# Differential attention: a score map in two PSUM tiles of two and three banks, a constant shift, casts on ACT, less filler per map

## The chip, the cores and the metric

One core of one Trainium2 chip runs the whole program. The metric is the device time of one execution in microseconds. Three executions of the kernel before took 4203.43 (median), 4199.43 and 4225.66 us.

## What is computed

Two layers of a block over 2048 latent and 256 context tokens of width 1024. In each layer one projection feeds four mixers side by side (differential attention, HGRN2, windowed attention with sinks, mLSTM) and a gate; their outputs, times the gate, go through an output projection and are added to the stream. The change lies in the differential attention. Cut to what matters:

```python
def attend(qs, ks, vs):                       # two maps m per head, 4 heads
    s = jnp.einsum('mbhqd,mbhkd->mbhqk', qs, ks).astype(F32) * scale
    p = jax.nn.softmax(s, axis=-1)
    w = (p[0] - lam * p[1]).astype(vs.dtype)
    return jnp.einsum('bhqk,bhkv->bhqv', w, vs)
...
o = lax.map(lambda qq: attend(qq, keys, vals), qb)   # blocks of 128 queries
y = from_heads(rmsnorm(o, g) * (1.0 - lam_init))
```

In the first layer the context tokens attend too (to themselves, 256 keys); in the last layer only the latent ones do, to all 2304 keys.

## The kernel before

Each layer runs in four stretches. First the tokens are normed, transposed and projected for the differential attention alone (`first_blocks`). Then comes the attention, with all other projections as filler for TensorE. Then what is left of the filler runs together with the first tiles of windowed attention and mLSTM (`rest_stream`, `swa_stream`, `mlstm_stream`). Last, HGRN's outputs and the output projection join them.

**A unit.** The attention goes through units: one head and one block of 128 queries. A full unit has 2304 keys, a context unit (two per head, first layer only) 256. Layer 0 has 64 full and 8 context units, layer 1 has 64 full ones. A unit does its two maps one after the other, map 1 first. For each map `diff_scores` writes 128 x 512 scores into one PSUM bank at a time (tile `scr`, a ring of five banks; five matmuls, the last with 256 columns), and VectorE takes each bank's maximum as soon as it is there (line 1048). A last small reduction makes the map's maximum, negated (line 1051). `diff_exp` then runs one exponential per bank on ACT, with the negated maximum as bias and the row sum as an accumulated output, into the SBUF tiles `p` (1024 and 1280 columns). A bank can take scores of the next map when its exponential has read it. For map 0 the bias also holds a term of map 1's row sum, through a reciprocal and a logarithm (lines 1040 to 1043 and 1053).

**Mixing.** `diff_mix` joins the maps a unit later: `p1 * factor + p0` on VectorE (line 1078), the float16 value of it on POOL (line 1080), the rest of it in float16 on POOL (line 1081), and a DMA that transposes both into `wt` (line 1083). It does one half (1024 or 1280 keys) per map. Its VectorE work is put right behind the operation that makes the bias (`issue_after(u["nm"].ins)`). `diff_out` multiplies `wt` by the values into tile `pv`, `diff_norm` scales and norms; they run one unit later again, on `u2` and `u3`.

**Filler.** `pump(ns)` runs steps of the other projections on TensorE until they are worth so many ns by the program's own count of columns. In `diff_scores` it is called after each bank but the last, with FSTEP; behind a map's scores and `diff_out`, with FGAP. Both stand at the end of a row of `ORDER_X`, one row a layer. TensorE's order in the attention is fixed by this code; the other engines' order is set by the scheduler. The filler (`other_blocks`) takes two queues side by side. The heavy one has mLSTM values, windowed keys and queries, mLSTM keys, and last the two gates of HGRN (`hgrn_gates`: twelve or more VectorE, ACT and POOL operations for each 24 pfm matmuls, and state matmuls `ktp` and `dS` behind them). The light one has plain projections and last the gate (`gate_silu`). A token-major projection writes `ptm` (256 columns a matmul), a feature-major one `pfm` (512).

**Behind the attention.** The streams are woven by a table of positions (`ORDER_Y`). While filler is left, windowed attention and mLSTM may only begin two tiles (`room`), since the other tiles' memory is still the projections'.

Of the kernel before, what the change touches and what calls it, by code (L numbers as in the profile page):

```python
# [22 lines left out]
    [33073.0, 2368.0, 1500.0, 1.0, 5637.0, 3547.0, 2, 9000.0, 2653.0, 15000.0, 1.15, 32192.0, 620.0, 2500.0],  # L23
    [29667.0, 2000.0, 2212.0, 1.0, 11215.0, 4000.0, 2, 9000.0, 4000.0, 22918.0, 1.15, 22000.0, 540.0, 2360.0],
# [9 lines left out]
P = 128  # L34
# [20 lines left out]
NEG = -1.0e30  # L55
ZLOW = -80.0
# [11 lines left out]
def kernel(  # L68
# [29 lines left out]
    def act(o, i, f, **kw):  # L98
        A.activation(out=o, in_=i, func=f, **kw)  # L99
# [152 lines left out]
    for l in range(n_layers):  # L252
# [63 lines left out]
        QSC = 32.0 ** -0.5  # L316
# [7 lines left out]
        alam = lp.tile([P, 1], F32, tag="alam", name=f"alam{l}")  # L324
# [11 lines left out]
        with tc.tile_pool(name=f"pa{l}", bufs=2, reuse_waits="tile", side="right" if l else "left") as pa, tc.tile_pool(name=f"pap{l}", bufs=4, space=PSUM, reuse_waits="tile") as pap:  # L336
# [9 lines left out]
            def layer_params():  # L346
# [28 lines left out]
                act(alam, lam, AF.Abs)  # L375
# [643 lines left out]
        with ExitStack() as st2:  # L1019
            da = st2.enter_context(tc.tile_pool(name=f"da{l}", bufs=2, reuse_waits="tile", side="right"))  # L1020
            sps = st2.enter_context(tc.tile_pool(name=f"sps{l}", bufs=1, reuse_waits="tile", space=PSUM, side="right"))
            KCH = [(0, 512), (512, 512), (1024, 512), (1536, 512), (2048, 256)]
            HALF = [(0, 1024), (1024, 1280)]

            def chunks_of(u):
                return [(2048, 256)] if u["ctx"] else KCH

# [3 lines left out]
            def diff_scores(u, m):  # L1031


                ch = chunks_of(u)
                sm = u["sm"]
                mx = sm[:, m * 5:m * 5 + len(ch)]
                pss = u["s", m] = []
                for j, (k0, n) in enumerate(ch):
                    if m == 0 and j == len(ch) - 1:
                        V.tensor_reduce(sm[:, 22:23], sm[:, 15:15 + len(ch)], AX.X, ALU.add)  # L1040
                        V.reciprocal(sm[:, 23:24], sm[:, 22:23])

                        act(sm[:, 24:25], sm[:, 23:24], AF.Ln, scale=alam, bias=one_t)
                    ps = sps.tile([P, 512], F32, tag="sc", name="scr", bufs=5)
                    mm(ps[:, :n], u["Qs"][:, m, u["qo"]:u["qo"] + P], u["Ks"][m][:, k0:k0 + n], True, True)
                    if j < len(ch) - 1:
                        pump(FSTEP * u["work"])
                    V.tensor_reduce(mx[:, j:j + 1], ps[:, :n], AX.X, ALU.max)  # L1048
                    pss.append(ps)
                nm = sm[:, 20 + m:21 + m]  # L1050
                u["nm"] = V.tensor_reduce(nm, mx, AX.X, ALU.max, negate=True)
                if m == 0:
                    u["nm"] = tt(V, nm, nm, sm[:, 24:25], ALU.subtract)

            def diff_exp(u, m):

                sm = u["sm"]
                pt = u[m] = [da.tile([P, 1280], F32, tag=f"p{m}", name=f"p{m}", bufs=4) for _ in halves_of(u)]
                for j, (k0, n) in enumerate(chunks_of(u)):
                    hf = 0 if u["ctx"] or k0 < 1024 else 1  # L1060
                    o = 0 if u["ctx"] else k0 - HALF[hf][0]
                    act(pt[hf][:, o:o + n], u["s", m][j][:, :n], AF.Exp, bias=sm[:, 20 + m:21 + m],
                        accum_out=sm[:, 10 + m * 5 + j:11 + m * 5 + j])

            def diff_mix(u, j):

                sm = u["sm"]
                if j == 0:
                    V.tensor_reduce(sm[:, 25:26], sm[:, 10:10 + len(chunks_of(u))], AX.X, ALU.add)
                    V.tensor_scalar(sm[:, 26:27], sm[:, 25:26], sm[:, 23:24], nlam, ALU.mult, ALU.mult)  # L1070
                    V.reciprocal(sm[:, 27:28], sm[:, 25:26])
                    u["w"] = []
# [5 lines left out]
                stt(p[:, :n], p[:, :n], sm[:, 26:27], u[0][j][:, :n], ALU.mult, ALU.add)  # L1078
                wl = u[0][j].bitcast(F16)
                G.tensor_scalar(wl[:, :n], p[:, :n], one_t, zero_t, ALU.mult, ALU.add)  # L1080
# [640 lines left out]
```

## Time and profile before

| what | us |
|---|---|
| median of 3 executions | 4203.43 |
| profiled execution, its own time | 4224.02 |
| its span, first to last instruction | 4222.2 |
| attention of layer 0 (first to last score matmul) | 238.3 to 1393 |
| attention of layer 1 | 2385 to 3432 |
| TensorE, VectorE, ACT, POOL busy | 3603.4, 3162.2, 2271.5, 2610.5 |

PE is TensorE's matmuls, PEld its weight loads, DVE is VectorE, ACT ScalarE, POOL GpSimd, SP the engine that issues most DMAs. Matmuls are pipelined, so the duration of one is longer than the distance to the next. A line such as L88 or L99 is a helper's; which part of the program it is is seen by the tile names. The granted clock is a share of full speed (2.4 GHz); at its lower level it is 1.2 GHz.

### The profile page before, as it was taken

The page shows a single profiled execution, that of the slowest core. Times are in us where ns is not written, and L with a number is a line of the kernel's source. Part 1 is how long each engine was busy: PE and PEld are TensorE (multiplying, and loading weights), DVE is VectorE, ACT ScalarE, POOL GpSimd, SP SyncE. Part 2 cuts the span into 40 slices and gives each one's busy share as a digit, 9 for nine tenths or more (in the row PEclk, how much of TensorE's full clock was granted, in tenths as well). Part 3 has the DMA queues.
Part 4 walks back from the last instruction along what each step waited for, and adds up shares of the span by engine and source line. Part 5 has one row for each costly group of instructions (what it writes and reads, how often), then busy time and mean ns, then how long its engine had stood idle before and what let it go on. Part 6 is the DMA issues. An engine that isn't in the chain of part 4 may idle for free. (4 is left out here: it accounts for less than half of the span.)

```text
span 4222.2 us, 82225 instructions
## 1 busy us (share of the span) xinstructions
PE 3603.4 (85%) x30342; PEld 2418.7 (57%) x30342; DVE 3162.2 (75%) x6137; ACT 2271.5 (54%) x6105; POOL 2610.5 (62%) x2037
## 2 busy tenths in 40 slices
PE   6999888887778878989998997899877678689998
PEld 3667564555555655655656585545555446556665
DVE  5167777789989776686743498888898986778774
ACT  5244555556666554565633355566666655545553
POOL 4455666555666676686647557775556766556663
PEclk9999899999999958898889999999989889588988
DMA  5357775765665675676644466668765656756662
GB/s 204 101 143 163 161 162 128 168 145 130 153 145 118 169 180 137 161 180 165 170 128 142 122 139 129 145 144 172 153 140 117 132 119 164 184 137 154 166 159 70
DMA packets 1256988, 622.42 MB, mean 147 GB/s; under 512 B 913476, under 2 KB 1203848, under 8 KB 1256584
## 3 DMA queue, kind: packets, MB, share of 16 engines
q1 hardware_dynamic: 1154216, 490.64, 51.8%
q10 hardware_dynamic: 102368, 126.52, 8.9%
q8 instruction: 239, 3.92, 0.4%
q14 instruction: 165, 1.35, 0.1%
HBM read 291.76 MB, written 131.23 MB: 100 GB/s over the span
## 5 line engine op out<-in xcount | busy, mean ns | idle before, releaser
L99 ACT ACTIVATE p<-scr,sm 128x512 f32<-128x512 f32 (+1 forms) x1296 | 814.5, 643 | 335.9 <-DVE sm L102 159.7
L1048 DVE TENSOR_REDUCE sm<-scr 128x1 f32<-128x512 f32 (+1 forms) x1296 | 785.1, 627 | 184.2 <-PE scr L88 175.0
L88 PE MATMUL pfm<-hh,wb 128*128 128x512 f16 (+1 forms) x2592 | 851.6, 376 | 49.6 <-ACT fm L99 12.9
L88 PE MATMUL ptm<-wb,hh 128*128 128x256 f16 (+2 forms) x5024 | 868.3, 276 | 25.5 <-DVE gz L105 7.9
L1080 POOL TENSOR_SCALAR p<-p,one_t,zero_t 128x1024 f16<-128x1024 f32 (+2 forms) x264 | 365.8, 1386 | 574.4 <-ACT p L99 296.4
L88 PE MATMUL ptm<-wb,hl 128*128 128x256 f16 (+2 forms) x2512 | 679.1, 275 | 2.5 <-POOL hl L102 2.4
L88 PEld LDWEIGHTS <-wb 128*128 128x128 f16 x3888 | 383.5, 102 | 519.2 <-issue 167.3
L88 PE MATMUL scr<-Ks,Qs 128*128 128x512 f16 (+1 forms) x1296 | 481.9, 379 | 194.2 <-ACT p L99 193.1
L88 PEld LDWEIGHTS <-hh 128*128 128x128 f16 x5024 | 486.5, 101 | 275.2 <-issue 154.7
L102 POOL TENSOR_TENSOR p<-p,p 128x1024 f16<-128x1024 f32 (+2 forms) x264 | 625.6, 2370 | 16.9
L88 PE MATMUL pfm<-hl,wb 128*128 128x512 f16 (+1 forms) x1296 | 488.2, 377 | 0.0
L105 DVE SCALAR_TENSOR_TENSOR p<-p,sm,p 128x1024 f32<-128x1024 f32 (+2 forms) x264 | 417.6, 1582 | 1.1
L88 PE MATMUL fx<-wo,mh 128*128 128x512 f16 x1088 | 375.5, 430 | 9.4 <-DVE xt L105 4.5
L88 PEld LDWEIGHTS <-hl 128*128 128x128 f16 x2512 | 253.5, 101 | 39.2 <-POOL hl L102 4.5
L88 PE MATMUL pv<-Vs,wt 128*128 128x128 f16 (+1 forms) x4640 | 244.1, 208 | 34.5 <-DMA wt<-p 25.5
L99 ACT ACTIVATION_READ_ACCUMULATOR p<-scr,sm 128x1 f32 x1296 | 267.4, 206 | 0.0
L102 POOL TENSOR_TENSOR ph<-swp,ph 128x640 f16<-128x640 f32 (+2 forms) x136 | 192.7, 1418 | 120.4 <-ACT ph L1322 100.5
L88 PEld LDWEIGHTS <-wt 128*128 128x128 f16 x4640 | 228.5, 99 | 60.3 <-DMA wt<-p 34.1
L88 PE MATMUL fx<-wo,mlo 128*128 128x512 f16 x544 | 233.3, 429 | 20.8 <-DVE mlo L102 20.6
L99 ACT ACTIVATE swp<-ss,ssm 128x640 f32<-128x640 f32 (+2 forms) x136 | 102.9, 756 | 176.5 <-DVE ssm L1318 164.7
L88 PEld LDWEIGHTS <-Qs 128*128 128x128 f16 x1296 | 131.2, 102 | 96.3 <-issue 24.2
L99 ACT ACTIVATE E<-E 128x1024 f32<-128x1024 f32 x119 | 124.8, 1052 | 88.0 <-POOL E L102 41.5
(304 smaller groups left out, 7331.9 us busy)
## 6 DMA issues: line engine op xcount, KB each, us to landing
wraw<-in_w_in_dram SPq DMA_DIRECT2D x60, 512.0 KB
dgt<-ga ACTq DMA_DIRECT2D x68, 256.0 KB
r1b<-dr SPq DMA_DIRECT2D x68, 256.0 KB
gtt<-dgt SPq DMA_DIRECT2D x34, 512.0 KB
mraw<-in_w_mod_dram SPq DMA_DIRECT2D x64, 256.0 KB
vi<-dhi SPq DMA_DIRECT2D x49, 256.0 KB
KSb<-dsk SPq DMA_DIRECT2D x56, 192.0 KB
Ks<-dka SPq DMA_DIRECT2D x64, 144.0 KB
```

The lines of the kernel that those rows point to most:

```text
L88: PE.matmul(o, lhsT=lhsT, rhs=rhs, start=start, stop=stop)
L99: A.activation(out=o, in_=i, func=f, **kw)
L102: return e.tensor_tensor(out=o, in0=a, in1=b, op=op)
L105: V.scalar_tensor_tensor(out=o, in0=a, scalar=s, in1=b, op0=op0, op1=op1)
L1048: V.tensor_reduce(mx[:, j:j + 1], ps[:, :n], AX.X, ALU.max)
L1080: G.tensor_scalar(wl[:, :n], p[:, :n], one_t, zero_t, ALU.mult, ALU.add)
```

## The change

Before, a map's scores lay in five tiles of one bank; now they lie in two tiles, one of two banks (1024 scores) and one of three (1280), with one reduction and one exponential each. Each tile has one buffer. The queries' scale is negative, so scores are negated: the reduction is a minimum, and the exponential has scale -1 and the minimum as bias, with no negation in between. Map 0's bias is shifted by a constant of the layer (`shf`, made once from lambda), where a term of map 1's row sum was. The sums, reciprocals and the factor are now made by three small operations in place of five and a logarithm on ACT. The float16 value of the mixed weights is made on ACT (`A.copy`), where it was a two-step scalar operation on POOL. FSTEP goes from 620 and 540 to 1100, and it is now used once a map, between the two tiles, where it was used four times.

```diff
 ORDER_X = [
-    [33073.0, 2368.0, 1500.0, 1.0, 5637.0, 3547.0, 2, 9000.0, 2653.0, 15000.0, 1.15, 32192.0, 620.0, 2500.0],
+    [33073.0, 2368.0, 1500.0, 1.0, 5637.0, 3547.0, 2, 9000.0, 2653.0, 15000.0, 1.15, 32192.0, 1100.0, 2500.0],
...
+RANGE = 32768.0
...
-        QSC = 32.0 ** -0.5
+        QSC = -32.0 ** -0.5
...
-                act(alam, lam, AF.Abs)
+
+                act(shf, lam, AF.Abs)
+                act(shf, shf, AF.Ln, scale=float(T), bias=one_t)
+                V.tensor_scalar(shf, shf, -1.0, math.log(RANGE), ALU.mult, ALU.add)
...
             def diff_scores(u, m):
...
-                for j, (k0, n) in enumerate(ch):
-                    if m == 0 and j == len(ch) - 1:
-                        V.tensor_reduce(sm[:, 22:23], sm[:, 15:15 + len(ch)], AX.X, ALU.add)
-                        V.reciprocal(sm[:, 23:24], sm[:, 22:23])
-
-                        act(sm[:, 24:25], sm[:, 23:24], AF.Ln, scale=alam, bias=one_t)
-                    ps = sps.tile([P, 512], F32, tag="sc", name="scr", bufs=5)
-                    mm(ps[:, :n], u["Qs"][:, m, u["qo"]:u["qo"] + P], u["Ks"][m][:, k0:k0 + n], True, True)
-                    if j < len(ch) - 1:
-                        pump(FSTEP * u["work"])
-                    V.tensor_reduce(mx[:, j:j + 1], ps[:, :n], AX.X, ALU.max)
-                    pss.append(ps)
-                nm = sm[:, 20 + m:21 + m]
-                u["nm"] = V.tensor_reduce(nm, mx, AX.X, ALU.max, negate=True)
-                if m == 0:
-                    u["nm"] = tt(V, nm, nm, sm[:, 24:25], ALU.subtract)
+                for j, (k0, n) in enumerate(hs):
+                    ps = sps.tile([P, 1536 if j else 1024], F32, tag=f"sc{j}", name="scr")
+                    for o in range(0, n, 512):
+                        w = min(512, n - o)
+                        mm(ps[:, o:o + w], u["Qs"][:, m, u["qo"]:u["qo"] + P], u["Ks"][m][:, k0 + o:k0 + o + w], True, True)
+                    if j < len(hs) - 1:
+                        pump(FSTEP * u["work"])
+                    V.tensor_reduce(sm[:, m * 2 + j:m * 2 + j + 1], ps[:, :n], AX.X, ALU.min)
+                    pss.append(ps)
...
+                if m:
+                    u["nm"] = tt(V, sm[:, 5:6], sm[:, o:o + 1], sm[:, o2:o2 + 1], ALU.min)
+                else:
+                    u["nm"] = V.tensor_scalar(sm[:, 4:5], sm[:, o:o + 1], sm[:, o2:o2 + 1], shf, ALU.min, ALU.add)
...
             def diff_exp(u, m):
...
+                    act(p[:, :n], u["s", m][j][:, :n], AF.Exp, scale=-1.0, bias=sm[:, 4 + m:5 + m],
+                        accum_out=sm[:, 6 + m * 2 + j:7 + m * 2 + j])
...
             def diff_mix(u, j):
...
-                    V.tensor_reduce(sm[:, 25:26], sm[:, 10:10 + len(chunks_of(u))], AX.X, ALU.add)
-                    V.tensor_scalar(sm[:, 26:27], sm[:, 25:26], sm[:, 23:24], nlam, ALU.mult, ALU.mult)
-                    V.reciprocal(sm[:, 27:28], sm[:, 25:26])
+                    zs = sm[:, 6:10].rearrange("p (m j) -> p m j", j=2)[:, :, :len(halves_of(u))]
+                    V.tensor_reduce(sm[:, 10:12], zs, AX.X, ALU.add)
+                    V.reciprocal(sm[:, 12:14], sm[:, 10:12])
+                    V.tensor_scalar(sm[:, 14:15], sm[:, 10:11], sm[:, 13:14], nlam, ALU.mult, ALU.mult)
...
-                G.tensor_scalar(wl[:, :n], p[:, :n], one_t, zero_t, ALU.mult, ALU.add)
+                A.copy(wl[:, :n], p[:, :n])
```

**TensorE, inside a map.** In layer 0's attention, before, TensorE's order has one score matmul (`scr`), the three matmuls that FSTEP pumps (here `pfm`, a feature-major projection: `hh` and `hl` are the two float16 parts of the tokens, `wb` the weights), and the next score matmul:

```order
L88 LDWEIGHTS Qs_0_12901
L88 MATMUL scr<-Ks_0_12891,Qs_0_12901 128x512
L88 LDWEIGHTS wb
L88 MATMUL pfm<-hh_1_132,wb 128x512
L88 LDWEIGHTS wb
L88 MATMUL pfm<-hl_1_133,wb 128x512
L88 LDWEIGHTS wb
L88 MATMUL pfm<-hh_1_132,wb 128x512
L88 LDWEIGHTS Qs_0_12901
L88 MATMUL scr<-Ks_0_12891,Qs_0_12901 128x512
```

Now the two matmuls of the first tile stand together, the pumped ones come once, and the three of the second tile follow (the first of them is shown):

```order
L89 LDWEIGHTS Qs_0_10317
L89 MATMUL scr<-Ks_0_10307,Qs_0_10317 128x512
L89 LDWEIGHTS Qs_0_10317
L89 MATMUL scr<-Ks_0_10307,Qs_0_10317 128x512
L89 LDWEIGHTS wb
L89 MATMUL pfm<-hh_3_136,wb 128x512
L89 LDWEIGHTS wb
L89 MATMUL pfm<-hl_3_137,wb 128x512
L89 LDWEIGHTS wb
L89 MATMUL pfm<-hh_3_136,wb 128x512
L89 LDWEIGHTS Qs_0_10317
L89 MATMUL scr<-Ks_0_10307,Qs_0_10317 128x512
```

Three of the four pumps inside a map are gone. Counted over TensorE's order between a layer's first and last score matmul, there stood 3141 ptm and 1512 pfm matmuls in layer 0 and 2784 and 1302 in layer 1; now 2160 and 1236, and 2064 and 1074. Of the 144 state matmuls `dS` of the HGRN gates 104 and 88 stood there, and now 16 and 16. The rest stands behind the last score matmul. In front of the last of it, 8 and 60 score matmuls of the windowed attention (`ss`, of 504 and 488) stood before, now 76 and 124.

**ACT, two maps.** Before, in layer 0's attention, ACT's order has the five exponentials of map 1 (`p_8278` and `p_8279` are its two halves), a projection's output (`rp`), the logarithm for map 0 and map 0's five exponentials:

```order
L99 ACTIVATE p_8278,sm<-scr,sm 128x512 x2
L99 ACTIVATE p_8279,sm<-scr,sm 128x512 x2
L99 ACTIVATE p_8279,sm<-scr,sm 128x256
L99 ACTIVATE rp<-pfm,bcol_116 128x512
L99 ACTIVATE sm<-sm,one_t,alam_124 128x1
L99 ACTIVATE p_8385,sm<-scr,sm 128x512 x2
L99 ACTIVATE p_8386,sm<-scr,sm 128x512 x2
L99 ACTIVATE p_8386,sm<-scr,sm 128x256
```

Now each map has two exponentials, and a cast of the unit before stands behind them:

```order
L100 ACTIVATE p_10390,sm<-scr,sm 128x1024
L100 ACTIVATE p_10392,sm<-scr,sm 128x1280
L100 ACTIVATE fm<-pfm,bcol_116 128x512
L586 DMA dhq_92<-fm 128x512
L1079 CAST p_10303<-p_10242 128x1024
L100 ACTIVATE p_10461,sm<-scr,sm 128x1024
L100 ACTIVATE p_10463,sm<-scr,sm 128x1280
L1079 CAST p_10305<-p_10244 128x1280
```

The casts came from POOL's order, the logarithm is gone, and ten exponentials a unit have become four.

## Rows read from the trace of the kernel before

**Rows 1.** The page, part 1: busy time, share of the span, instructions.
```profile
PE 3603.4 (85%) x30342; PEld 2418.7 (57%) x30342; DVE 3162.2 (75%) x6137; ACT 2271.5 (54%) x6105; POOL 2610.5 (62%) x2037
```

**Rows 2.** Stretches: length, busy us PE, PEld, DVE, ACT, POOL, clock, DMA share, GB/s.
```profile
238.30:1003.00 764.70, 671.79 (x5860) 445.81 (x5859) 611.34 (x1294) 412.51 (x1180) 450.27 (x287) 0.95 0.66 151
1003.00:1393.00 390.00, 311.26 (x2688) 215.50 (x2688) 365.93 (x726) 251.10 (x659) 255.69 (x164) 0.93 0.60 139
1393.00:1475.00 82.00, 68.38 (x647) 52.74 (x646) 52.14 (x102) 40.29 (x96) 48.54 (x43) 0.97 0.74 179
2385.00:3088.00 703.00, 616.61 (x5396) 414.79 (x5395) 618.31 (x1254) 410.95 (x1165) 455.40 (x278) 0.96 0.67 144
3088.00:3432.00 344.00, 251.84 (x2099) 167.23 (x2096) 313.16 (x601) 215.36 (x561) 222.35 (x143) 0.88 0.57 127
3432.00:3540.00 108.00, 83.21 (x619) 55.95 (x618) 76.25 (x139) 57.75 (x135) 71.04 (x55) 0.84 0.63 162
3540.00:3585.00 45.00, 43.00 (x399) 36.01 (x397) 22.95 (x48) 23.85 (x58) 23.76 (x23) 1.00 0.53 135
```

**Rows 3.** Tile scr in layer 1's first and layer 0's second part.
```profile
L88 PE MATMUL scr<-Ks,Qs x465: 269/379/634, 2385.2 to 3087.6; 128*128 128x512 f16 x124, 128*128 128x256 f16 x31
...
L88 PE MATMUL scr<-Ks,Qs x208: 272/379/634, 1006.1 to 1392.3; 128*128 128x512 f16 x82, 128*128 128x256 f16 x22
```

**Rows 4.** Waits in layer 1's attention: who for whom, us, times, longest us.
```profile
PE scr L88 <- ACT p L99: 111.4, 61, 9.8
ACT p L99 <- DVE sm L102: 75.9, 48, 4.0
DVE sm L1048 <- PE scr L88: 75.5, 129, 6.3
```

**Rows 5.** Groups by form in layer 1's attention: count, busy us, mean ns, idle before.
```profile
L99 ACT ACTIVATE p<-scr,sm 128x512 f32<-128x512 f32 x508 | 342.3, 685 | 151.8 <-DVE sm L102 75.9 <-DVE sm L1051 35.0 <-DVE sm L1069 24.2
L1048 DVE TENSOR_REDUCE sm<-scr 128x1 f32<-128x512 f32 x508 | 335.8, 682 | 75.1 <-PE scr L88 72.8
...
L1080 POOL TENSOR_SCALAR p<-p,one_t,zero_t 128x1280 f16<-128x1280 f32 x62 | 91.2, 1471 | 137.6 <-ACT p L99 73.5 <-DVE p L105 63.3 <-ACT dCs L881 0.7
...
L99 ACT ACTIVATE p<-scr,sm 128x256 f32<-128x256 f32 x127 | 61.7, 485 | 0.0
...
L1048 DVE TENSOR_REDUCE sm<-scr 128x1 f32<-128x256 f32 x127 | 52.6, 414 | 3.9 <-PE scr L88 2.7
...
L99 ACT ACTIVATE sm<-sm,one_t,alam 128x1 f32<-128x1 f32 x63 | 24.3, 386 | 41.1 <-DVE sm L1041 39.3 <-POOL sp L102 1.5
...
L99 ACT ACTIVATE wb<-wraw 128x1024 f16<-128x1024 f32 x20 | 21.3, 1064 | 21.0 <-DMA wraw<-in_w_in_dram 11.9 <-POOL sp L102 4.9 <-issue 4.2
L102 DVE TENSOR_TENSOR sm<-sm 128x1 f32<-128x1 f32 x63 | 20.7, 329 | 5.7 <-ACT sm L99 1.1 <-DVE sm L1051 0.5
...
L1051 DVE TENSOR_REDUCE sm<-sm 128x1 f32<-128x5 f32 x127 | 19.5, 154 | 2.6
```

**Rows 6.** Timeline, layer 1: start us, us, engine and operation [idle before].
```profile
2900.78 0.38 PE L88 MATMUL pfm<-hh,wb 128*128 128x512 f16 x1
...
2900.99 0.38 PE L88 MATMUL pfm<-hl,wb 128*128 128x512 f16 x1
...
2905.63 2.81 DVE L1048 TENSOR_REDUCE sm<-scr 128x1 f32<-128x512 f32 x5
...
2909.40 0.68 ACT L99 ACTIVATE p<-scr,sm 128x512 f32<-128x512 f32 x1
...
2910.07 0.69 ACT L99 ACTIVATE p<-scr,sm 128x512 f32<-128x512 f32 x1
...
2911.39 0.49 ACT L99 ACTIVATE p<-scr,sm 128x256 f32<-128x256 f32 x1
...
3553.63 0.38 PE L88 MATMUL ptm<-wb,hh 128*128 128x256 f16 x2
...
3553.96 0.38 PE L88 MATMUL ptm<-wb,hh 128*128 128x256 f16 x2
```

More of the change, by code (lines that the diff above doesn't have):

```diff
@@ L323 @@
         nlam = lp.tile([P, 1], F32, tag="nlam", name=f"nlam{l}")
-        alam = lp.tile([P, 1], F32, tag="alam", name=f"alam{l}")
+        shf = lp.tile([P, 1], F32, tag="alam", name=f"shf{l}")
         hst = ExitStack()
@@ L1055, in diff_exp @@
+                o2 = o + len(hs) - 1
+                if m:
+                    u["nm"] = tt(V, sm[:, 5:6], sm[:, o:o + 1], sm[:, o2:o2 + 1], ALU.min)
+                else:
+                    u["nm"] = V.tensor_scalar(sm[:, 4:5], sm[:, o:o + 1], sm[:, o2:o2 + 1], shf, ALU.min, ALU.add)
             def diff_exp(u, m):
                 sm = u["sm"]
[L1058 to L1063, printed above, removed]
+                pt = u[m] = []
@@ L1065, in diff_mix @@
+                for j, (k0, n) in enumerate(halves_of(u)):
+                    p = da.tile([P, 1280], F32, tag=f"p{m}", name=f"p{m}", bufs=4)
+                    act(p[:, :n], u["s", m][j][:, :n], AF.Exp, scale=-1.0, bias=sm[:, 4 + m:5 + m],
+                        accum_out=sm[:, 6 + m * 2 + j:7 + m * 2 + j])
+                    pt.append(p)
             def diff_mix(u, j):
@@ L1077, in diff_mix @@
                 p = u[1][j]
-                stt(p[:, :n], p[:, :n], sm[:, 26:27], u[0][j][:, :n], ALU.mult, ALU.add)
+                stt(p[:, :n], p[:, :n], sm[:, 14:15], u[0][j][:, :n], ALU.mult, ALU.add)
                 wl = u[0][j].bitcast(F16)
-                G.tensor_scalar(wl[:, :n], p[:, :n], one_t, zero_t, ALU.mult, ALU.add)
+                A.copy(wl[:, :n], p[:, :n])
                 tt(G, wl[:, n:2 * n], p[:, :n], wl[:, :n], ALU.subtract)
@@ L1109, in diff_norm @@
                     ot = u["ot"] = da.tile([P, 64], F32, tag="ot", name="ot")
-                    act(ot, pv[:, 64:128], AF.Copy, scale=sm[:, 27:28])
+                    act(ot, pv[:, 64:128], AF.Copy, scale=sm[:, 12:13])
                     return
@@ L1115, in diff_norm @@
                 oall = head["o"]
-                stt(oall[:, i], pv[:, 0:64], sm[:, 27:28], ot, ALU.mult, ALU.add)
+                stt(oall[:, i], pv[:, 0:64], sm[:, 12:13], ot, ALU.mult, ALU.add)
                 if i == nq - 1:
@@ L1146, in units @@
                                        work=CTXW if ctx_ else 1.0, of=(i, 2) if ctx_ else (qt % 8, 8),
-                                       sm=da.tile([P, 28], F32, tag="sm", name="sm", bufs=5))
+                                       sm=da.tile([P, 16], F32, tag="sm", name="sm", bufs=5))
             owed = [0.0]
```

10 lines of the change are left out of this document (3 added, 7 removed).

## The prediction

> **What bounds the kernel now.** I read the page's engine shares first, then the stretches, then the groups by form inside the attention of layer 1, then the waits, and last the timeline of a few units. The shares over the whole span say little: TensorE 85%, VectorE 75%, no engine full [rows 1]. The stretches say more [rows 2]. Attention runs from 238 to 1393 us in layer 0 and from 2385 to 3432 us in layer 1, 1154.7 and 1047.0 us, together 52% of the span. A unit (one head, one block of 128 queries, two maps) has ten score matmuls, so 656 in the code of layer 0 are 65.6 units and 640 are 64. A layer's attention has two parts. While the filler is plain projections, TensorE is busy 88% in both layers (671.8 of 764.7 us; 616.6 of 703.0 us) and VectorE 80% and 88%. Once the filler is the HGRN gates (from 1003 and 3088 us), VectorE is busy 94% and 91% and TensorE falls to 80% and 73%, with a granted clock of 0.88 in the second. By the score matmuls in the two parts [rows 3] a unit takes 15.1 us in layer 1's first part (46.5 units) and 19.7 us in its second (17.5 units); VectorE's work is 13.3 and 17.9 us a unit. In layer 0 it is 13.6 (44.8 units) and 17.6 us (20.8 units). So TensorE and VectorE share the bound first, VectorE holds it later. The waits show the chain between them [rows 4]: in layer 1 TensorE stands 111.4 us in front of score matmuls until an exponential has emptied a bank, ACT 75.9 us in front of one map's exponentials for the small VectorE operation that makes their bias, VectorE 75.5 us for scores.
>
> **The change, part by part.**
>
> *Maxima.* A 512-column reduction takes 682 ns and a 256-column one 414 ns [rows 5]: 1.047 ns a column and 146 ns fixed. The trace has no 1024 or 1280; on that line they take 1218 and 1486 ns. A unit had 8 x 0.682 + 2 x 0.414 = 6.28 us, now 2 x (1.218 + 1.486) = 5.41 us: -0.87 us by durations. Five in a row took 2.81 us, where their durations add to 3.14 us [rows 6], so 0.08 us of each overlaps the next and the six that go save only some 0.4 us. The bounds are -0.4 and -0.9. Of the small VectorE operations, which take from 0.15 us (a map's last reduction) to 0.33 us (the subtraction) [rows 5], eight become five: at 0.15 us each -0.45 us. Together I take -1.0 us a unit: 66 us of VectorE in layer 0, 64 in layer 1.
>
> The Trainium skill (Perfetto Trace Analysis, Optimizing Scalar/DVE Operations) gives VectorE about 125 ns fixed for an operation on PSUM, with a profiled duration that holds about twice the busy part, since the tail overlaps the next instruction. The 146 ns line with 0.08 us overlapped has the same shape; by 125 ns the six would give -0.75 us, inside the bounds.
>
> *Exponentials and casts on ACT.* Exponentials back to back start 0.66 us apart for 512 columns, the accumulator read included, and the 256 one takes 0.49 us [rows 6]: a map takes 4 x 0.66 + 0.49 = 3.1 us. Durations of 685 and 485 ns [rows 5] give 0.78 ns a column, so 1024 and 1280 take 0.66 + 0.40 = 1.06 and 1.26 us: 2.3 us, -0.8 a map, -1.6 a unit. The logarithm goes, -0.39. The cast of 1024 float32 to float16 takes 1.064 us on ACT, as the weights show [rows 5], so 1.26 for 1280: +2.3 us. Net +0.3 us a unit on an engine that is busy 58% and 63% in layer 1's two parts [rows 2]: nothing in the sum while the casts stand beside VectorE's work, priced in the rivals if not. POOL loses two casts a unit, the longer one 1.47 us [rows 5]; it is busy about 65%, and what it makes is read a turn of the unit loop later (`diff_out` of `u2` and `u3`), so that too counts nothing.
>
> *The chain of a map.* Only two tiles hold a map, so from bias to bias there stand: the 1024 exponential (1.06), the 1280 one (1.26), three matmuls (0.22 us apart [rows 6], 0.7), the 1280 minimum (1.49) and the combination (at most the 0.33 of the subtraction): 4.8 us, with hand-overs of 0.05 to 0.1 us some 5.1 us, 10.2 us a unit. That is under what TensorE and VectorE need below, so it adds waits but sets no pace.
>
> *Fewer fillers.* Per map the pumped work goes from 4 x 620 + 2500 = 4980 ns to 1100 + 2500 = 3600 (layer 1: 4520 to 3460). In the order this takes 981 ptm and 276 pfm matmuls out of layer 0's attention, 720 and 228 out of layer 1's. They stand 0.109 and 0.216 us apart where nothing waits (three ptm in 0.33 us) [rows 6]. That is 167 and 128 us of TensorE, moved behind the attention, not removed. With it goes most of the HGRN gate work: 16 state matmuls stay in either attention, of 104 and 88.
>
> *New attention time.* TensorE: 671.8 + 311.3 - 167 = 816 us in layer 0 and 616.6 + 251.8 - 128 = 740 in layer 1. At the 88% that it reaches when the filler is plain, 927 and 841 us. VectorE: what the gates added over ordinary filler is (17.6 - 13.6) x 20.8 = 82 us and (17.9 - 13.3) x 17.5 = 80 us; it leaves, with the 66 and 64 above. 977 - 66 - 82 = 829 and 931 - 64 - 80 = 787 us; at the 91% of its fullest part in layer 1, 911 and 865 us. The later of each pair: 927 and 865 us, 14.1 and 13.5 us a unit. Saved: 1155 - 927 = 228 and 1047 - 865 = 182, together 410 us.
>
> *What the moved filler costs behind it.* The 295 us run after the last scores. There TensorE was busy 83% (1393 to 1475 us), 77% at a clock of 0.84 while layer 1's attention drains, and 96% at full clock in the middle of that remainder [rows 2]. The drain is paid now as well, and the middle grows, so I take 93%: 180 + 138 = 318 us. Bounds: 307 us (96%) and 383 us (77%).
>
> *Work pulled forward.* In the order 68 and 64 more score matmuls of the window attention stand in front of the last projection than before, some two tiles a layer. The stretch from 3585 us to the end is 637 us for 16 tiles, 40 us each; if a quarter of that is what was pulled forward, four tiles give -40 us, but they need VectorE in the longer remainder too. Bounds -40 and 0, taken -20.
>
> Sum: -410 + 318 - 20 = -112 us. The profiled run took 4224.0 us, 20.6 above the median of 4203.4; from the median the forecast is 4091 us, 2.7% faster.
>
> **Rivals.**
>
> *The attention is freed more* (faster still). If VectorE no longer holds the units once the gates' work has left them, a unit nears what TensorE alone needs, 12.5 and 11.6 us, held up by the chain: 12.6 us a unit in both layers, 827 and 806 us, saving 569. -569 + 318 - 20 = -271: 3932 us. For it: 111 us of bank waits and the 19.7 us units. Against: two tiles hold fewer scores than five banks, so TensorE runs less far ahead.
>
> *Only moved.* TensorE keeps its present share of the attention, 983 / 1155 = 85% and 868 / 1047 = 83%: 960 and 892 us, 350 saved; the remainder runs at 83% too, 355 us, and nothing is pulled forward. +5: 4208 us. For it: all matmuls are still there and TensorE is the longest row of the page. Against: the stalls at the gates are VectorE's.
>
> *The coarse tiles stall the map* (slower). Place: ACT's queue in the attention. The chain is 5.1 us only if the cast and ACT's filler fall into its gaps. ACT is busy 411 us in 46.5 units, 8.8 a unit, of which 2 x 3.1 + 0.39 + 0.31 are attention's; 0.95 us a map is filler. With cast (1.16) and filler in front of the exponentials and one filler operation of 0.68 us on VectorE in front of the last minimum, a map takes 5.1 + 1.16 + 0.95 + 0.68 = 7.9 us, a unit 15.7: 1030 and 1005 us, saving 167 against 318 - 20. +131: 4334 us. It decides from 14.7 us a unit, where the saving is eaten up. For it: five small steps that let banks free one by one become two. Against: in the order the cast stands behind both exponentials of its map, and its VectorE input is issued right behind the bias, so it should fall into VectorE's reductions.
>
> The Trainium skill speaks for this rival (Perfetto Trace Analysis, Optimizing Scalar/DVE Operations): larger operations pay where an engine is saturated, and breaking them up pays where it only causes bubbles on others. The bank waits are such bubbles and ACT is not saturated, so by this rule the merged exponential should lengthen them; no run here shows it yet. VectorE at 88% to 94% is the saturated case of the same rule.
>
> **How the numbers follow.** Forecast 0.50, freed more 0.20, only moved 0.17, stalled 0.13. A measurement of this kernel tells about 1% from no change: 42 us, so faster means under 4161. The forecast's own spread (one unit time off by 0.5 us is 65 us) leaves it there 9 times in 10: 0.45 + 0.20 + a quarter of "only moved" is 0.69. Same: 0.05 + 0.12, some 0.18 with the stalled case's near end; slower 0.13. The range goes from just above the freed case, 3950, to past "only moved" and its bounds of the remainder, 4235.
>
> **What would show it.** Attention of 927 and 865 us, units of 14.1 and 13.5; the reductions at 1.2 and 1.5 us; bank waits no larger than 111 us in layer 1; the remainder longer by 180 and 138 us; VectorE's busy time down by some 130 us in all. It is wrong if units stay over 14.7 us, or if the remainder runs below 77% TensorE.

## The result, and the profile after

The kernel after takes 4277.23 us (median of 4 executions, 4262.31 to 4286.93), the kernel before 4207.45 us on the same chip (4 executions): a ratio of 1.0155, 95% interval 1.0132 to 1.0177. It is 1.6% slower, where 2.7% faster was forecast, and it lies above the range. The profiled execution's span is 4281.7 us, 59.5 more than before.

The page of the kernel after, part 1, as [rows 1]:

```profile
PE 3613.9 (84%) x30342; PEld 2414.4 (56%) x30342; DVE 3066.6 (72%) x4963; ACT 2329.5 (54%) x4699; POOL 2246.3 (52%) x1773
```

VectorE has 95.6 us less to do and POOL 364, TensorE the same (10.5 us more, on matmuls that are the same in number). Busy time that goes does not make time go by itself; TensorE's idle time has grown. Where, the stretches say, as [rows 2]: the attention, what is left of the filler behind it up to the last state matmul `dS`, and the rest up to the output projection's last matmul (in layer 1 to the end of the span), in layer 0 and then in layer 1 (columns: length, then busy us of PE, PEld, DVE, ACT, POOL, the clock, DMA share, GB/s):

```profile
237.00:1245.60 1008.60, 811.27 (x7077) 531.74 (x7076) 844.49 (x1246) 597.74 (x985) 454.43 (x260) 0.94 0.67 150
1245.60:1544.90 299.30, 276.39 (x2320) 207.59 (x2320) 159.27 (x340) 155.51 (x330) 141.74 (x126) 0.96 0.51 137
1544.90:2253.70 708.80, 621.12 (x5397) 411.16 (x5392) 470.28 (x870) 372.45 (x1015) 460.85 (x471) 0.81 0.62 157
...
2417.80:3324.30 906.50, 723.23 (x6362) 475.05 (x6361) 808.64 (x1131) 571.78 (x890) 444.41 (x243) 0.95 0.67 144
3324.30:3665.90 341.60, 288.44 (x2311) 209.17 (x2310) 208.16 (x374) 182.84 (x363) 168.51 (x143) 0.89 0.51 133
3665.90:4281.70 615.80, 547.28 (x4722) 360.25 (x4720) 446.99 (x816) 309.07 (x868) 347.73 (x338) 0.79 0.53 137
```

The same six stretches of the kernel before, cut at the same matmuls:

```profile
238.30:1393.20 1154.90, 983.25 (x8550) 661.48 (x8549) 977.47 (x2019) 663.82 (x1839) 706.16 (x450) 0.95 0.64 147
1393.20:1473.80 80.60, 67.89 (x646) 52.36 (x643) 51.19 (x100) 39.80 (x94) 47.14 (x42) 0.98 0.74 180
1473.80:2216.90 743.10, 653.87 (x5597) 435.09 (x5594) 503.89 (x937) 395.07 (x1099) 489.94 (x502) 0.81 0.64 160
...
2385.20:3432.40 1047.20, 868.65 (x7490) 582.12 (x7489) 931.87 (x1855) 626.30 (x1725) 678.15 (x420) 0.93 0.64 139
3432.40:3590.30 157.90, 128.94 (x1040) 94.29 (x1038) 102.94 (x192) 84.71 (x198) 96.94 (x79) 0.88 0.59 151
3590.30:4222.20 631.90, 553.69 (x4866) 373.90 (x4862) 465.29 (x852) 321.95 (x901) 362.39 (x351) 0.81 0.58 145
```

So the two attentions got 287 us shorter (2202.1 to 1915.1) and everything behind them 352 us longer (1613.5 to 1965.5; the remainders +402, the rest -50). TensorE did 317 us less in the attentions and 329 more behind them, and it stood idle 381 us in the attentions, where it was 350, and 232 us behind them, where it was 209. The removed filler took about its own length with it and none of the idle time.

The waits in layer 1's attention, as [rows 4] (who for whom: us, times, longest us):

```profile
POOL p L103 <- ACT p L1079: 355.9, 99, 11.4
...
PE scr L89 <- ACT p L100: 148.1, 110, 6.7
DVE sm L1043 <- PE scr L89: 77.5, 116, 4.7
ACT p L100 <- DVE sm L1068: 74.7, 45, 4.2
ACT p L100 <- DVE sm L1051: 57.5, 31, 3.7
...
ACT p L100 <- DVE sm L103: 25.2, 14, 3.2
```

POOL's subtraction now waits for the cast on ACT. TensorE waits longer for exponentials (148 us, was 111), and ACT waits for the small VectorE operations that make the bias. L1068 is not one of them: it is a sum that stands right behind map 1's combination, and the wait is put down to whichever came last. The groups by form in the same stretch, as [rows 5]:

```profile
L1043 DVE TENSOR_REDUCE sm<-scr 128x1 f32<-128x1280 f32 x127 | 188.9, 1487 | 52.6 <-PE scr L89 52.1
...
L103 POOL TENSOR_TENSOR p<-p,p 128x1280 f16<-128x1280 f32 x62 | 162.3, 2618 | 171.1 <-ACT p L1079 161.7 <-issue 9.4
L1043 DVE TENSOR_REDUCE sm<-scr 128x1 f32<-128x1024 f32 x128 | 156.1, 1219 | 26.8 <-PE scr L89 25.4
...
L1079 ACT CAST p<-p 128x1280 f16<-128x1280 f32 x62 | 77.8, 1255 | 1.0 <-DVE p L106 0.9
...
L103 DVE TENSOR_TENSOR sm<-sm 128x1 f32<-128x1 f32 x64 | 56.8, 887 | 0.1
...
L1051 DVE TENSOR_SCALAR sm<-sm,shf 128x1 f32<-128x1 f32 x63 | 16.9, 269 | 1.3
```

The reductions (1.487 and 1.219 us) and the cast (1.255) are as forecast. The surprise is the `sm<-sm` TENSOR_TENSOR: map 1's combination, one element per partition from two others, takes 887 ns on average, 639 in layer 0. Map 0's, a TENSOR_SCALAR of the same size, takes 269. The timeline shows why (start, length, engine and operation, in brackets the idle time before it):

```profile
3060.37 1.49 DVE L1043 TENSOR_REDUCE sm<-scr 128x1 f32<-128x1280 f32 x1 [0.61 <-PE scr L89]
3060.39 2.61 POOL L103 TENSOR_TENSOR p<-p,p 128x1280 f16<-128x1280 f32 x1 [3.64 <-ACT p L1079]
3061.97 1.04 DVE L103 TENSOR_TENSOR sm<-sm 128x1 f32<-128x1 f32 x1
...
3063.11 1.11 ACT L100 ACTIVATE p<-scr,sm 128x1024 f32<-128x1024 f32 x1 [0.55 <-DVE sm L1068]
...
3064.21 1.32 ACT L100 ACTIVATE p<-scr,sm 128x1280 f32<-128x1280 f32 x1
3064.37 0.59 PE L89 MATMUL scr<-Ks,Qs 128*128 128x512 f16 x2 [1.24 <-ACT p L100]
...
3066.09 0.70 PE L89 MATMUL scr<-Ks,Qs 128*128 128x512 f16 x3
...
3066.83 1.49 DVE L1043 TENSOR_REDUCE sm<-scr 128x1 f32<-128x1280 f32 x1 [0.61 <-PE scr L89]
3068.36 0.27 DVE L1051 TENSOR_SCALAR sm<-sm,shf 128x1 f32<-128x1 f32 x1
...
3068.72 1.11 ACT L100 ACTIVATE p<-scr,sm 128x1024 f32<-128x1024 f32 x1 [2.16 <-issue]
...
3073.03 2.61 POOL L103 TENSOR_TENSOR p<-p,p 128x1280 f16<-128x1280 f32 x1 [4.28 <-ACT p L1079]
...
3073.62 2.04 DVE L103 TENSOR_TENSOR sm<-sm 128x1 f32<-128x1 f32 x1
...
3075.75 1.11 ACT L100 ACTIVATE p<-scr,sm 128x1024 f32<-128x1024 f32 x1 [2.57 <-DVE sm L1068]
```

Two things are to be seen. The combination at 3061.97 ends at 3063.01, where POOL's subtraction ends (3060.39 + 2.61 = 3063.00); that at 3073.62 ends at 3075.66, POOL's at 3075.64. Of 136 combinations 84 took over 0.4 us; all 84 began inside a POOL TENSOR_TENSOR and ended with it. The 41 that began while POOL was idle took 0.15 us on average. Map 0's combination, which takes its second element as a scalar operand, began inside a POOL operation 91 times and never took more than 277 ns. And from 3063.11 to 3068.72 the chain of a map stands in full: exponential, two score matmuls 0.15 us after its end, filler, three score matmuls, minimum, combination, next exponential: 5.61 us without a hold.

The Trainium skill (SBUF — State Buffer, Who interferes with whom) says it as a rule: a VectorE operation with two SBUF inputs and a GpSimd operation that reads SBUF exclude each other, and the one that starts second waits for the whole of the first; a reduction never does. The trace agrees with the first half by the 84 held ones, and the run with a reduction below agrees with the second: there 94 of 136 reductions began inside a POOL operation, and the longest took 156 ns. The prediction did not draw on that section.

### The profile page after: what moved, and what is told of

It reads as the page before. It is cut to its first block, busy times and chain, and to the rows that moved or that the text cites. A ratio compares the mean times of both kernels' runs of the same rounds, so it can differ in the third digit from the quotient of the medians.

```text
span 4281.7 us, 79313 instructions
## 1 busy us (share of the span) xinstructions
PE 3613.9 (84%) x30342; PEld 2414.4 (56%) x30342; DVE 3066.6 (72%) x4963; ACT 2329.5 (54%) x4699; POOL 2246.3 (52%) x1773
## 5 line engine op out<-in xcount | busy, mean ns | idle before, releaser
L89 PE MATMUL ptm<-wb,hh 128*128 128x256 f16 (+2 forms) x5024 | 833.9, 273 | 30.5 <-DVE dSs L106 9.1
L100 ACT ACTIVATE p<-scr,sm 128x1024 f32<-128x1024 f32 (+2 forms) x528 | 628.4, 1194 | 423.0 <-DVE sm L1068 149.4
L1043 DVE TENSOR_REDUCE sm<-scr 128x1 f32<-128x1024 f32 (+2 forms) x528 | 698.6, 1326 | 205.7 <-PE scr L89 201.5
L89 PE MATMUL pfm<-hh,wb 128*128 128x512 f16 (+1 forms) x2592 | 811.5, 377 | 26.4 <-DVE gz L106 7.1
L89 PE MATMUL scr<-Ks,Qs 128*128 128x512 f16 (+1 forms) x1296 | 362.5, 379 | 276.9 <-ACT p L100 272.0
L1079 ACT CAST p<-p 128x1024 f16<-128x1024 f32 (+2 forms) x264 | 297.4, 1127 | 36.5 <-DVE p L106 32.2
L89 PEld LDWEIGHTS <-wt 128*128 128x128 f16 x4640 | 240.3, 102 | 72.2 <-DMA wt<-p 26.4
L89 PE MATMUL pv<-Vs,wt 128*128 128x128 f16 (+1 forms) x4640 | 255.1, 212 | 23.1 <-DMA wt<-p 17.4
L103 DVE TENSOR_TENSOR rp<-rp,cs 128x512 f32<-128x512 f32 (+1 forms) x64 | 80.8, 1265 | 134.0 <-POOL rt L103 120.5
L89 PE MATMUL gA<-QQ,KK 64*64 64x64 f32 x3808 | 129.8, 251 | 47.7 <-DVE QQ L103 30.9
```

The lines of the kernel that those rows point to most:

```text
L89: PE.matmul(o, lhsT=lhsT, rhs=rhs, start=start, stop=stop)
L103: return e.tensor_tensor(out=o, in0=a, in1=b, op=op)
L1043: V.tensor_reduce(sm[:, m * 2 + j:m * 2 + j + 1], ps[:, :n], AX.X, ALU.min)
L1079: A.copy(wl[:, :n], p[:, :n])
```

## The experiments

Theory A: the moved filler costs more than it frees, and the held combination stands on the path of map 1. Its rivals: B, the coarse tiles stall the map; C and D, filler costs by its place or by its length; E, the casts on ACT hold up exponentials. Each ratio is against the kernel before on the same chip (medians of 4204 to 4211 us), so runs are better compared by ratios than by microseconds; two ratios have to differ by some 0.3 to 0.5% to be clear of the noise.

### Combination as a reduction, and filler back between the tiles

```diff
-u["nm"] = tt(V, sm[:, 5:6], sm[:, o:o + 1], sm[:, o2:o2 + 1], ALU.min)
+u["nm"] = V.tensor_reduce(sm[:, 5:6], sm[:, o:o2 + 1], AX.X, ALU.min)
```

> The kernel after, with one edit: map 1's combination (the smaller of two one-element minima) is a reduction over the two neighbouring elements, where it is an operation with two SBUF inputs that took 639 ns (layer 0) and 887 ns (layer 1) on average. Theory A (moved filler, and besides it a combination held by POOL on the path of map 1): the operation falls to 0.15 to 0.2 us, 0.45 us for each of 72 units and 0.7 us for each of 64 units leave the attention, 77 us if all of it is on the path, about half if the waits shift to the next late thing: 4200 to 4240 us, all of it in the attention. Theory B (the two coarse single-buffered tiles stall the map by themselves): the operation gets shorter, but the bank waits stay near 148 us in layer 1's attention and the time stays at 4265 to 4285 us.

Measured 4220.53 us, ratio 1.0033 (1.0014 to 1.0052): 1.2% (some 50 us) faster than the kernel after, by one operation of one element per partition a unit. Its row in layer 1's attention:

```profile
L1049 DVE TENSOR_REDUCE sm<-sm 128x1 f32<-128x2 f32 x64 | 9.2, 144 | 0.2
```

Attentions 1869.8 us, 45 less; theory A put the gain there. Another 26 us of the profiled difference lie in the rests, which have the same matmuls at a granted clock of 0.83 and 0.82 where it was 0.81 and 0.79; why is not shown. Theory A has its second half; what is left, 0.3%, is no gain either. The next three ask about the filler. Each changes the last two numbers, FSTEP and FGAP, of the two rows of `ORDER_X`. The kernel after with full filler, as much as before:

```diff
-    [33073.0, ... 32192.0, 1100.0, 2500.0],
-    [29667.0, ... 22000.0, 1100.0, 2360.0],
+    [33073.0, ... 32192.0, 2480.0, 2500.0],
+    [29667.0, ... 22000.0, 2160.0, 2360.0],
```

> The kernel after, with FSTEP 2480 (layer 0) and 2160 (layer 1), once a map: as much filler per map as the kernel before has. Theory A (the moved filler costs more behind the attention than it frees in it): the remainders shrink back to some 82 and 158 us, the attention grows back by 290 to 340 us, and the time is that of the kernel before within 1%, 4170 to 4240 us. Theory B (the tiles stall the map, whatever the filler): the time stays above the kernel before by the same 1.5% or more, 4265 us and up, since the tiles are still there. A third reading (TensorE only waits in the attention and filler is free there): the attention stays near 1009 and 907 us and the time falls below 4050 us.

4255.09 us, 1.0112 (1.0082 to 1.0143): 0.4% below after, hardly clear of the noise, and still over before. A's 4240 was too low, B's 4265 too high. The kernel before with as little filler as after:

```diff
-    [33073.0, ... 32192.0, 620.0, 2500.0],
-    [29667.0, ... 22000.0, 540.0, 2360.0],
+    [33073.0, ... 32192.0, 275.0, 2500.0],
+    [29667.0, ... 22000.0, 275.0, 2360.0],
```

> The kernel before (five banks, ten exponentials a unit, casts on POOL), with FSTEP 275 in both layers: as little filler per map as the kernel after. Theory A: moving the filler alone does it: 50 to 80 us slower than before, 4255 to 4290 us, remainders near 300 and 340 us. Theory B (it is the tiles): the same as before within 1%, or faster, 4110 to 4240 us.

4266.16 us, 1.0142 (1.0108 to 1.0176). Moving the filler alone makes the kernel before as slow as the change does. Two tiles with the reduction (1.0033) are 1.1% faster at the same small filler, so B does not hold there. With five banks, too, the attentions get 306 us shorter (1895.9) and all behind them 348 longer. Then both edits of the kernel after together, the reduction and FSTEP 2480 and 2160:

> Both edits: the kernel after with the combination as a reduction, and with as much filler per map as before. Theory A: the two add, 4277 - 60 - (40 to 77) = 4140 to 4180 us, faster than the kernel before by 1 to 1.5%. Theory B: at or above the kernel before, 4200 us and up. If with more filler in a map the combination is hidden behind TensorE, it is no faster than the run with the filler alone.

4231.31 us, 1.0054 (1.0027 to 1.0080). The two don't add: A's sum of 4140 to 4180 is refuted. Here the whole of a map's FSTEP stands in one place, between the two tiles, and so inside the chain that the timeline shows.

### Where filler stands, and where the cast runs

All three are the kernel after with the reduction, and one more edit. Full filler, the added part behind the map:

```diff
-    [33073.0, ... 32192.0, 1100.0, 2500.0],
-    [29667.0, ... 22000.0, 1100.0, 2360.0],
+    [33073.0, ... 32192.0, 1100.0, 3880.0],
+    [29667.0, ... 22000.0, 1100.0, 3420.0],
```

> The kernel after with map 1's combination as a reduction, and with as much filler per map as the kernel before, but the added part stands behind the map: FSTEP stays 1100, FGAP is 3880 (layer 0) and 3420 (layer 1). Theory C (a map goes round a chain of two exponentials, score matmuls, minimum and combination, and filler between the two tiles stands in that chain, while filler behind the map fills the time in which TensorE waits for the exponentials): those waits are 118.6 us in 810 us of layer 1, about 1.0 us a map, so of 1.4 us more filler a map some 0.4 us lengthens it; attention near 1930 us for both layers together, remainders back to 85 and 150 us: 3920 to 4050 us. Theory D (TensorE and VectorE are simply used up, filler costs its own time wherever it stands): as with the filler between the tiles, 4200 to 4250 us.

4168.97 us, 0.9905 (0.9877 to 0.9933): faster than before, 62 us faster than with the same filler between the tiles. Place matters (C); but the attentions are 2180.6 us, 311 longer than with less filler, for some 320 us more of TensorE: filler behind the map is not free either (D), and C's 3920 to 4050 is far off. The filler of after, none of it between the tiles:

```diff
-    [33073.0, ... 32192.0, 1100.0, 2500.0],
-    [29667.0, ... 22000.0, 1100.0, 2360.0],
+    [33073.0, ... 32192.0, 0.0, 3600.0],
+    [29667.0, ... 22000.0, 0.0, 3460.0],
```

> The kernel after with map 1's combination as a reduction, and with the same filler per map as it has, but none of it between the two tiles: FSTEP 0, FGAP 3600 and 3460. Theory C: the score matmuls of a map take some 1.6 to 1.9 us from first to last where they take 2.43 (the second tile then waits for the second exponential), 0.5 to 0.8 us of 128 maps and more leave the attention unless TensorE gets no more to wait: 4120 to 4190 us. Theory D: as the kernel with the combination alone within 1%, or slower because TensorE now stands idle in front of the second tile: 4200 to 4260 us.

4231.99 us, 1.0047 (1.0027 to 1.0068), no clear difference from 1100 between the tiles (1.0033): the score matmuls of a map now span 1.9 us on average in layer 1, where it was 2.7, but the next map's first one comes 0.75 us after the exponential that frees its tile, where it came 0.27, since TensorE's filler in front of it got longer. The float16 cast back on POOL:

```diff
-A.copy(wl[:, :n], p[:, :n])
+G.tensor_scalar(wl[:, :n], p[:, :n], one_t, zero_t, ALU.mult, ALU.add)
```

> The kernel after with map 1's combination as a reduction, and with the float16 cast back on POOL. Theory C (the chain of a map, casts beside it): the casts on ACT cost at most the few exponentials that they are in front of, 4190 to 4240 us, the same within 1%. Theory E (the casts on ACT hold up exponentials and, through them, the tiles): each map gets 0.3 to 1 us shorter, 4090 to 4180 us. If the cast had been a help because POOL is short of time, slower: over 4260 us.

4257.08 us, 1.0110 (1.0072 to 1.0149): slower by 0.8% than the same with the cast on ACT, just under the 4260 named for that case. E is refuted: with the combination as a reduction the cast on ACT is a gain.

### The hold by itself, and the best place of the filler

The kernel after with FSTEP 1100 and FGAP 3880 and 3420, as above, but its combination left as it is:

> The kernel after with as much filler per map as the kernel before, the added part behind the map (FGAP 3880 and 3420), and map 1's combination left as it is, with two SBUF inputs. Theory A (that operation, held by POOL, is on the path of map 1 in any case, worth 57 us where the filler was short): 4169 + 40 to 60 = 4210 to 4230 us. Theory F (with TensorE filled, the path of map 1 has slack and the hold is hidden): 4165 to 4190 us.

4201.69 us, 0.9985 (0.9966 to 1.0004): 0.8% (33 us) above the same with the reduction, between A and F. With little filler the hold cost 1.2%; that it costs less with TensorE filled is not clear of the noise. Now POOL's subtraction as a one-input operation, in the kernel after:

```diff
-tt(G, wl[:, n:2 * n], p[:, :n], wl[:, :n], ALU.subtract)
+G.tensor_scalar(wl[:, n:2 * n], p[:, :n], one_t, zero_t, ALU.mult, ALU.add)
```

> The kernel after, but POOL's two-input subtraction (value minus its float16 value) is a one-input scalar operation of the same size; this leaves the low half of the mixed weights out of the computation, and POOL's operation falls from 2.6 and 2.2 us to some 1.5 and 1.2 us. Theory A (map 1's combination is held by POOL's running two-input operation): the combination, unchanged, falls from 887 and 639 ns to 0.15 to 0.35 us, and the time to 4200 to 4240 us, as with the reduction. Theory G (the one-element operation with two SBUF inputs is slow by itself): it stays over 0.6 us, and the time at 4250 to 4285 us.

4158.32 us, 0.9880 (0.9850 to 0.9910). Layer 1's attention:

```profile
L106 DVE SCALAR_TENSOR_TENSOR p<-p,sm,p 128x1280 f32<-128x1280 f32 x62 | 101.1, 1630 | 0.0
L1080 POOL TENSOR_SCALAR p<-p,one_t,zero_t 128x1280 f16<-128x1280 f32 x62 | 93.6, 1510 | 179.9 <-DVE p L106 115.4 <-ACT p L100 52.8 <-DVE gates L632 4.7
...
L103 DVE TENSOR_TENSOR sm<-sm 128x1 f32<-128x1 f32 x64 | 15.7, 245 | 0.2
```

The unchanged combination falls from 887 to 245 ns (268 in layer 0), so G falls: it is POOL's operation that makes it long. But the second input on POOL is not what holds it. Four combinations began inside POOL's one-input operation, and all four were held to its end, for 0.65 to 1.26 us; two were held so in the kernel before, by its one-input cast. One of the four:

```profile
593.63 1.41 POOL L1080 TENSOR_SCALAR p<-p,one_t,zero_t 128x1280 f16<-128x1280 f32 x1 [4.70 <-DMA Qs<-dqa]
...
594.14 0.91 DVE L103 TENSOR_TENSOR sm<-sm 128x1 f32<-128x1 f32 x1
```

What the edit changed is that POOL was seldom at work at that moment: 24 of the 136 began inside any POOL operation, where it was 95. The time went below the 4200 to 4240 named. Of the further 62 us against the run with the reduction, 59 lie in the attentions. There VectorE's SCALAR_TENSOR_TENSOR, the 704 of either run, add up to 579 us for 631. Those that mix the maps have two SBUF inputs too: in either run they take 1.54 us (1280 columns) and 1.28 us (1024) where POOL is idle, and 1.6 to 2.0 us on average where they begin inside a POOL operation. So POOL makes them longer; that this is the whole of the 59 us is argued, not tried by itself.

Less between the tiles at full filler (with the reduction):

```diff
-    [33073.0, ... 32192.0, 1100.0, 2500.0],
-    [29667.0, ... 22000.0, 1100.0, 2360.0],
+    [33073.0, ... 32192.0, 700.0, 4280.0],
+    [29667.0, ... 22000.0, 700.0, 3820.0],
```

> Combination as a reduction, as much filler per map as before, less of it between the two tiles: FSTEP 700, FGAP 4280 and 3820. Theory C (the chain still sets the pace part of the time): 0.2 to 0.4 us a map less, 4115 to 4150 us. Theory D (TensorE sets it): 4155 to 4185 us, the same as with 1100 between the tiles.

4151.14 us, 0.9871 (0.9842 to 0.9901): 18 us (0.3%) less than with 1100 between them, which is not clear of the noise, and between the two answers. It has the lowest time here of the kernels that compute all of the reference. TensorE's wait for exponentials in layer 1's attention is half that of the kernel after:

```profile
PE scr L89 <- ACT p L100: 75.5, 48, 7.7
```

More filler still (with the reduction):

```diff
-    [33073.0, ... 32192.0, 1100.0, 2500.0],
-    [29667.0, ... 22000.0, 1100.0, 2360.0],
+    [33073.0, ... 32192.0, 1100.0, 4300.0],
+    [29667.0, ... 22000.0, 1100.0, 3800.0],
```

> Combination as a reduction, FSTEP 1100, and still more filler behind the map: FGAP 4300 and 3800 (layer 0 and 1), some 50 us of TensorE more in the two attentions. If filler goes on costing less in the attention (1.05 us for one of TensorE) than behind it (1.2 us): 4150 to 4165 us. If the time in which TensorE waited is used up, or the filler runs out before the attention ends: 4170 to 4210 us.

4210.94 us, 0.9999 (0.9984 to 1.0013): the attentions grow by 108 us, and in layer 0 the filler is used up 38 us before the last score. Now the kernel before with its filler behind the map:

```diff
-    [33073.0, ... 32192.0, 620.0, 2500.0],
-    [29667.0, ... 22000.0, 540.0, 2360.0],
+    [33073.0, ... 32192.0, 175.0, 4280.0],
+    [29667.0, ... 22000.0, 175.0, 3820.0],
```

> The kernel before (five banks, ten exponentials a unit, casts on POOL) with the same filler per map, most of it behind the map: FSTEP 175 four times, FGAP 4280 and 3820, the same sums as the run of two tiles with 700 between them (4151 us). It asks whether the two tiles bring anything once filler and combination are set right. If the gain there is only the filler's place: 4140 to 4175 us, the same as the two tiles. If the tiles are worth the 1.0 us of VectorE per unit that was forecast, or the five banks want their filler between them: 4190 to 4230 us, as the kernel before.

4247.10 us, 1.0085 (1.0054 to 1.0117). Five banks want their filler between them; two tiles, with the rest of the change and the reduction, are 2.1% faster with most of it behind the map (0.9871 / 1.0085 = 0.979). Each at its best place here, they are 1.3% faster (0.9871 against the kernel before). So the change has a gain in it. Last, why the hold became so frequent; the kernel after with only the cast back on POOL (the same diff as above):

> The kernel after, with the float16 cast back on POOL and nothing else changed: map 1's combination keeps its two SBUF inputs. It asks why the combination is held so often now (84 of 136 times), where its counterpart before was held 35 of 136 times. If the cast on ACT is the reason (it ends right behind the second exponential and lets POOL's subtraction start just before the combination): the combination's mean falls from 639 and 887 ns to 0.3 to 0.45 us, and the time is within 25 us of the run with the reduction and the cast on POOL (4257 us), 4250 to 4280 us. If POOL's subtraction meets the combination wherever the cast runs: the mean stays over 0.6 us, and the time is 4290 to 4320 us.

4276.54 us, 1.0168 (1.0140 to 1.0197). In layer 1's attention:

```profile
L103 DVE TENSOR_TENSOR sm<-sm 128x1 f32<-128x1 f32 x64 | 31.6, 494 | 0.1
```

The mean is 494 ns (455 in layer 0), above what the first answer named and below the second; 45 of 136 are over 0.4 us, where it was 84. So about half of the hold came with the cast on ACT, which ends behind the second exponential and lets POOL's subtraction start during the last minimum. The time fits the first answer: the gain of the cast and the hold that it brings about cancel.

## Why the prediction was wrong

*What adds up.* Forecast were -410 us in the attentions, +318 in the remainders and -20 in the rest: -112. Measured were -287, +402 and -50, +65, and 5 us less elsewhere. So 123 us of the miss lie in the attentions and 54 behind them. One path from before to after, in ratios: the new tiles, casts and small operations with full filler, most of it behind the map, and a free combination -0.95%; the two-input combination +0.8% (0.9905 to 0.9985); less filler +1.7% (0.9985 to 1.0155). The forecast had the last as the gain and the second as nothing.

*Maxima.* Right in size: 1219 and 1487 ns for 1218 and 1486 forecast; VectorE's busy time is 146 us lower with the reduction (3016.3), for 130 forecast. In the kernel after the hold ate 50 of it.

*Exponentials and casts on ACT.* Nearly right: 1.32 and 1.11 us an exponential in the timeline (1.26 and 1.06 forecast), 1.255 and 1.042 us a cast, beside other work, and better than on POOL. What it moved was not costed: "nothing in the sum" held for ACT, but the subtraction behind the cast came to lie on the combination.

*Chain of a map.* Wrong in two terms. The combination was priced "at most the 0.33 of the subtraction"; it took 0.64 and 0.89 us, up to 2.3. The trace of before had the warning: its subtraction took 329 ns for one element where a small reduction took 154 [rows 5]; 35 of its 136 were over 0.4 us, 33 of them inside a POOL TENSOR_TENSOR and two inside POOL's cast, while the 91 that began with POOL idle took 158 ns. A mean over a few long ones was read as a bound. And the score matmuls were counted as 0.7 us, where the filler of FSTEP stands between them: they span 2.4 in the timeline above. The second exponential, beside them, made up for part: 5.6 us for 5.1, without a hold.

*Fewer fillers.* 295 us were forecast to move; 317 left the attentions by TensorE's busy time.

*New attention time.* This is the step that failed. It let TensorE rise to the 88% of its best stretch, and VectorE to 91%, once the gates' work had left. That makes TensorE's idle time in the attentions 1792 - 1556 = 236 us. TensorE's work came out as forecast, 811 and 723 us for 816 and 740, but its share fell to 80% in both layers, and it stood idle 381 us where it had been 350. Units took 15.4 and 14.2 us for 14.1 and 13.5; the first is over the 14.7 that the prediction named as its sign of being wrong. Moving the filler alone, with five banks, shows the same (the first pair of lines has the two attentions of the kernel before with less filler, the second pair those of the kernel after with the reduction and full filler behind the map; columns as above):

```profile
235.20:1225.70 990.50, 820.98 (x7090) 530.18 (x7089) 847.43 (x1843) 582.02 (x1686) 625.91 (x394) 0.94 0.71 153
...
2392.40:3297.80 905.40, 745.58 (x6362) 479.90 (x6361) 814.12 (x1705) 553.99 (x1590) 617.12 (x370) 0.94 0.68 144
```

```profile
234.30:1379.10 1144.80, 984.06 (x8710) 669.13 (x8708) 915.95 (x1441) 689.41 (x1152) 543.31 (x325) 0.96 0.66 150
...
2349.50:3385.30 1035.80, 860.72 (x7465) 581.16 (x7464) 876.44 (x1290) 645.99 (x1028) 518.84 (x298) 0.93 0.63 140
```

TensorE's idle time is 329 us in the first pair and 336 in the second; two tiles with the reduction and less filler have 348. In all 15 profiles it lies between 298 and 396 us, 2.3 to 3.1 us a unit (129.6 units). It is lowest with POOL's operation of one input (298) and with 700 between the tiles (300), and highest with full filler between the tiles and the hold (396). Taking filler out did not bring it near 236 in any of them. The holds and the place of the filler seem to move it more than the amount does, but the same 30342 matmuls add up to anything from 3546 to 3621 us of busy time in these profiles, so differences of some 40 us in idle time say little. A us of filler taken out is about a us saved: 287 us for 317 here, 306 for 285 with five banks. That is 287 us where 410 were forecast.

*Moved filler behind.* The remainders grew by 402 us (bound 383, taken 318), the rest got 50 shorter (taken 20): 352 for 298. TensorE's work in the remainders grew by 368 us, the 317 from the attentions and some 39 that the rest lost, where 295 were taken; it ran at 92% and 84% for 93%. No run changes the weave behind the attention (`ORDER_Y`), so it is not shown whether the moved filler could cost less there. In layer 1's remainder TensorE waits 31 us for POOL's part of the HGRN gates:

```profile
PE ktp L96 <- POOL ke L103: 30.7, 6, 10.5
```

*Rivals.* "Only moved" came nearest: its 350 us saved are 332 in the run with the free combination, and its 4208 us nearly that run's 4221. The agreement in the total is partly luck: it had the remainders 355 us longer and nothing pulled forward, where in that run they grew by 397 and the rest got 76 shorter. "The coarse tiles stall the map" does not hold where filler is short (1.0033 against 1.0142) or behind the map (0.9871 against 1.0085); with all of the full filler between the tiles, two tiles are 0.5% slower than five banks (1.0054 against the kernel before). The rule cited for it (the Trainium skill, Perfetto Trace Analysis, Optimizing Scalar/DVE Operations), that breaking operations up helps where they make bubbles, is not borne out by the time. Bank waits rose, from 111 to 148 us in layer 1, but less filler alone raised them with five banks too:

```profile
PE scr L88 <- ACT p L99: 127.4, 106, 9.3
```

With two tiles and the reduction they are 134 us, so most of the rise is the filler and the hold.

Still open: why TensorE keeps some 300 us and more of idle time in the attentions at any amount of filler that was tried, and whether the longer SCALAR_TENSOR_TENSOR explain all of the one-input run's extra gain.

## What to carry to other kernels

Do not count on filler that is taken out of a stretch and run elsewhere to shorten the stretch by much more than its own length, unless a run shows that TensorE's idle time goes with it: cost the move at zero and look for what is lost behind. Place the filler anew when the tiles change: here two tiles with full filler wanted it behind the map (1.5% faster than between the tiles), and five banks wanted it between them (0.9%). Before a small operation is put on a chain, look at its single durations, not the mean, and at what POOL does at that moment; a form with one SBUF input did the same here in 144 ns (a reduction over two neighbours) and was not held once.

## What the hardware showed

A VectorE operation on one element per partition, with two SBUF inputs, took up to 2.3 us in the kernel after, because POOL was in the middle of an operation of 2.6 us; with POOL idle it took 0.15 us. POOL's one-input operations held it as well (0.65 to 1.26 us in the one-input run). The same combination as a reduction took 144 ns on average and 156 at most. Removing the holds was worth 1.2% where TensorE had little filler and 0.8% where it had as much as before.
